# Low parts of the second halves by accumulating transfers, and eight more pieces by seven products, in an encoder block

## The chip, the cores and the metric

The kernel runs on one core of one Trainium2 chip. The metric is the time of one execution in microseconds of the device; what is compared is the median over several runs.

## The reference

One encoder block on 256 tokens of width 2048, in float32:

```
h    = rms_norm(x) @ w_in                       # q, k, v of two attentions, and two gates
ya   = windowed_gqa(...)   ; yb = dilated_attention(...)
x    = x + (sigmoid(ga) * (ya @ w_branch_a) + sigmoid(gb) * (yb @ w_branch_b)) @ w_out
hf   = rms_norm(x)
x    = x + (gelu(conv3(hf @ w_ffn_gate)) * (hf @ w_ffn_up)) @ w_ffn_down     # d_ff 5632
x    = x + sigmoid(rms_norm(x) @ w_ple_gate) * (p @ w_ple_proj)
out  = rms_norm(x)
```

Nearly all of the work is products of 256 rows with weight matrices, whose float32 weights are read from memory once.

## The kernel before, in words

**Pieces, units, parts.** The weights lie in memory as 258 pieces of 1 MB (128 partitions by 2048 float32). Each is loaded by SP (`load`) into one of three buffers `raw`. A matrix product is made from split operands: a float32 operand is written as a high part, rounded to the type that TensorE takes, and a low part, the rest; a product then is three matmuls, high by high, high by low, low by high (`thirds`, L408 to L410). ACT makes the high part of the weights (L305, an `ACTIVATE` Copy into `uh` or `vh`) and DVE the low part (L306, raw less high, into `ul` or `vl`). This is done by `produce`, a unit at a time; a unit is half a piece or less. Plain units go to rings of six slots (`uh`, `ul`), units of weight sums to rings of two (`vh`, `vl`). `drop` gives a slot back when the last product that reads it has been written, and `pump` then produces what has become possible, so production is some three pieces ahead of use.

**Stages.** A: input projection and attention. B0 to B3: the two gates, 512 columns of each at a time, with the branch projections ba and bb behind each. D0, D1: output projection. E0, E1: up and gate projections of the two halves of the inner width. F00, F01, F10, F11: down projections. pp0, pp1, G0, G2, G3: the embedding at the end. In A and E the weights are the stationary operand (L351, L358), and each piece takes 32 matmuls. In B, D, F and G0 (the quad stages) a piece is a 2 by 2 arrangement of 128x512 blocks, times 2 by 2 blocks of activations. A piece is of one of these kinds, given by a letter in the strings `FIRST_GATES` (B0), `ALT` (B1 to B3, D, and G0 with Z for S) and `DOWN` (F0, F1):

- `s`: by eight block products, 24 matmuls.
- `S`: by seven (Winograd's form of Strassen's method), 21 matmuls. DVE forms the sums of weight blocks in place in `raw` (L295 to L297), and sums of activation blocks are made once and kept (`combine`, `sums_of`). Its units are a first quarter, a second half, and two units of sums.
- `Z`: by seven, with one sum of weights made beforehand: POOL loads three blocks by halves (`sum_ahead`, L268), DVE adds (L271, L272), POOL stores (L275), all during E0 and E1, and the later load fetches 768 KB of the piece and 256 KB of the sum. DVE does L282 and L283 in place.
- `w`: branch projections, and G2 and G3, by plain products, 24 matmuls.

A planner sets the order of instructions on each engine before the run; it may put ready matmuls ahead of others. What is wrapped in `keep` stays in program order on its engine. `at(stage, ...)` and `run_due` hang side work (sums of activations, row sums, transposes) at places in the product order.

Of the kernel before, what the change touches and what calls it, by code (L numbers as in the profile page):

```python
# [16 lines left out]
P = 128  # L17
# [74 lines left out]
WIDE = 2 * T  # L92
_JOBS = _plan()
NA = len(_JOBS)
ALT = "SsSsSsSs"
DOWN = ("ZZsZsZsZsZs", "ZsZsZsZsZss")
LASTS = 30
ASK, ADD, STORE = 0, 12, 13
FIRST_GATES = "ssssSsSs"


def _ffn(half):
# [65 lines left out]
def _unit_list():  # L168

    units, of = [], []  # L170
    for p, (kind, _) in enumerate(_PIECES):
        if p == 0:
            cuts = [("n", a * P, b * P) for a, b in ((0, 1), (1, 4), (4, 7), (7, 11), (11, PIECE))]
        elif kind == "Z":
            cuts = [("n", WIDE, 2 * WIDE), ("n", 2 * WIDE, 4 * WIDE), ("T21", 0, 2 * WIDE), ("T03", 2 * WIDE, 4 * WIDE)]
        elif kind == "S":
            cuts = [("n", 0, WIDE), ("n", 2 * WIDE, 4 * WIDE), ("T13", 0, 2 * WIDE), ("T24", 2 * WIDE, 4 * WIDE)]
        else:
            cuts = [("n", 0, 2 * WIDE), ("n", 2 * WIDE, 4 * WIDE)]
        of.append(list(range(len(units), len(units) + len(cuts))))  # L180
        units += [(p, *cut) for cut in cuts]
    return units, of


_UNITS, _UNITS_OF = _unit_list()
_FBLOCKS = [(u, o) for p, (kind, _) in enumerate(_PIECES) if kind == "f" for u in _UNITS_OF[p]
            for o in range((_UNITS[u][3] - _UNITS[u][2]) // P)]
_LAST_OF = {u: o for u, o in _FBLOCKS}
# [5 lines left out]
def _encoder(ctx: ExitStack, tc, xt, pt, xrow, cols, gainrow, table, onehot, mask, ident_in, wts, out):  # L194
# [84 lines left out]
    def sums_of_weights(raw):  # L279

        q = [raw[:, i * WIDE:(i + 1) * WIDE] for i in range(4)]
        nc.vector.tensor_tensor(q[1], q[0], q[1], op=ALU.subtract)  # L282
        nc.vector.tensor_tensor(raw[:, 2 * WIDE:], raw[:, 2 * WIDE:], view(q[0], 0, (0, 2), (1, WIDE)), op=ALU.subtract)  # L283

    def produce():

        u = state["unit"]
        p, kind, a, b = _UNITS[u]
        while state["raw"] < min(p + 3, _NPIECES):
            load(state["raw"])  # L290
        raw = raws[p]
        ring = "u" if kind == "n" else "v"
        if kind == "T13":
            q = [raw[:, i * WIDE:(i + 1) * WIDE] for i in range(4)]
            nc.vector.tensor_tensor(raw[:, :2 * WIDE], raw[:, WIDE:3 * WIDE], raw[:, :2 * WIDE], op=ALU.subtract)  # L295
            nc.vector.tensor_tensor(q[2], q[2], q[0], op=ALU.subtract)
            nc.vector.tensor_tensor(q[3], q[3], q[2], op=ALU.subtract)  # L297
        behind = _PIECES[p][0] == "Z" == _PIECES[p - 1][0]
        if kind == "T21" and not behind:
            sums_of_weights(raw)  # L300
        src = raw[:, a:b]
        pool = wpool if ring == "u" else held["tok"]
        hi = pool.tile([P, b - a], FR, name=ring + "h", bufs=RINGS[ring])
        lo = pool.tile([P, b - a], FR, name=ring + "l", bufs=RINGS[ring])
        nc.scalar.activation(hi, src, AF.Copy)  # L305
        nc.vector.tensor_tensor(lo, src, hi.bitcast(F32), op=ALU.subtract)  # L306
        if behind and u == _UNITS_OF[p][1]:
            sums_of_weights(raw)
        made[u] = (hi, lo)
        state["unit"] = u + 1  # L310
        state[ring] -= 1
# [275 lines left out]
    def at(i, f, *a):  # L587

        due.setdefault(i, []).append((f, a))
# [320 lines left out]
    def sums_of(u, tag, s=None):  # L910

        tok = held["tok"]
        f = tok.tile([P, 4, P], F32, name="cmb")
        x11, x21, x12, x22 = (u[:, k, t * P:(t + 1) * P] for k in range(2) for t in range(2))
        nc.vector.tensor_tensor(f[:, 0], x21, x22, op=ALU.add)
        nc.vector.tensor_tensor(f[:, 2], x11, x21, op=ALU.subtract)
        nc.vector.tensor_tensor(f[:, 1], f[:, 0], x11, op=ALU.subtract)
        nc.vector.tensor_tensor(f[:, 3], x12, f[:, 1], op=ALU.subtract)
        if s is None:
            s = tok.tile([P, 2, 4, P], FR, name="S", tag="S%d" % tag)  # L920
        nc.scalar.activation(s[:, 0], f, AF.Copy)
        nc.vector.tensor_tensor(s[:, 1], f, s[:, 0].bitcast(F32), op=ALU.subtract)
        return s
# [36 lines left out]
        return h  # L960

    at(("B0", 3, 0), open_tok)
    for i, when in ((4, (3, 1)), (6, (3, 6)), (0, (5, 2)), (2, (7, 2))):
        at(("B0", *when), combine, "hs", hs, i, i // 2)
    rh = halved(rc[0])

    for j in range(4):

        def gated(t, n, a):
            c = held["c"][t][:, cut[n]]  # L970
            nc.vector.tensor_tensor(c, a, c, op=ALU.add)
            a = c
            nc.scalar.activation(c, a, AF.Tanh, scale=rh[:, t:t + 1])

        if j == 1:
            at(("ba1", 0, 0), combine, "merged", held["merged"], 0, 4)
        if j == 3:
            at(("B3", 2, 4), combine, "merged", held["merged"], 2, 0)
            at(("B3", 4, 4), combine, "merged", held["merged"], 4, 1)
        quads("B%d" % j, lambda k: hs[:, k, :], lambda i: combos["hs", i], gated)  # L980
        if j == 0:
            held["merged"] = big.tile([P, KC, 2 * T], FR, name="merged", tag="R1")
        c = held["c"]
        for half, (stage, y, names) in enumerate((("ba%d" % j, lambda k: ya[:, k, :], ("M1", "M6")), ("bb%d" % j, yb.get, ("M7", "M5")))):
            accs = wide_stage(stage, y, names)
            for t in range(2):
                m = c[t][:, cut[half]]
                nc.vector.scalar_tensor_tensor(m, m, 1.0, accs[t], op0=ALU.add, op1=ALU.mult)
                if half:
                    nc.vector.tensor_tensor(c[t][:, cut[0]], c[t][:, cut[0]], m, op=ALU.add)  # L990
        merged_turns("B%d" % (j + 1) if j < 3 else "D0", j, c)
# [7 lines left out]
    def residual(stage, s, moving, key, square):  # L999

        wide = slice(2 * s * WIDE, 2 * (s + 1) * WIDE)

        def finish(t, n, a):
            r = xr[:, t, cut[2 * s + n]]
            nc.vector.tensor_tensor(r, r, a, op=ALU.add)
            if n:
                nc.vector.tensor_tensor(xr[:, t, wide], xr[:, t, wide], held["c"][t], op=ALU.add)
            if n and square:
                nc.scalar.activation(held["c"][t], xr[:, t, wide], AF.Square,
                                     accum_out=held["ssq"][:, s, t:t + 1])  # L1010

        quads(stage, moving, lambda i: combos[key, i], finish)
# [127 lines left out]
    for half in range(2):  # L1140
        held["act"], held["places"] = {}, places(half)
        jobs = _ffn(half)
        joint = 0 if half else JOINT
        stage = "E%d" % half
        accs = [bank(which) for which in ("M1", "M5", "M6", "M7")[:joint]]
        if joint:
            products(stage, lambda k: hf[:, k, :], KC, accs)
        for (kind, n), a in zip(jobs, accs):
            mlp(kind, n, a)
        turns["e"] = 0  # L1150
        todo = [(p, h) for p in sevens(half) for h in range(2)]
        for i, (kind, n) in enumerate(jobs[joint:]):
            if i > 1 and todo and (i % 2 == 0 or i < LASTS):
                held["job"] = todo.pop(0), ("act2", "S4")[i % 2]
                one_ahead(stage)
            finish_ahead(stage)
            mlp(kind, n, product(stage, lambda k: hf[:, k, :], KC, "e"))
        assert not todo
        drain_ahead()
        if half:  # L1160
            at(("F10", 2, 0), load_last)
            at(("F10", 9, 0), split_last)
            held["ssq"] = sc.tile([P, 2, 2], F32, name="ssq", bufs=1)
        residual("F%d0" % half, 0, activation_row, "act", half)
        if half:
            pl = big.tile([P, KC, 2 * T], FR, name="pl", tag="R0")
            for pair, when in enumerate((("F11", 0, 6), ("F11", 1, 2), ("F11", 1, 5), ("F11", 2, 1))):
                at(when, rows_pair, "P22", pair, pl, 2)
            at(("F11", 2, 4), combine, "pl", pl, 0, 0)
            at(("F11", 4, 4), combine, "pl", pl, 2, 1)  # L1170
        residual("F%d1" % half, 1, activation_row, "act", half)


# [8 lines left out]
        held["rp"] = halved(rows_root())  # L1182

    at(("pp1", 0, 0), ple_root)
    at(("pp1", 0, 4), combine, "pl", pl, 4, 2)
    at(("G0", 1, 4), combine, "pl", pl, 6, 3)
    names = ("M1", "M6", "M7", "M5")

    class Rows:
# [118 lines left out]
```

## Time and profile before

| | |
|---|---|
| times of three runs | 1455.38, 1455.40, 1455.77 us |
| median | 1455.4 us |
| span of the profiled execution (first to last instruction) | 1453.7 us |
| TensorE matmuls | 7470 |
| pieces by seven in B0, B1 to B3, D0, D1, G0 | 2, 4 each, 4, 4, 4 |
| pieces by seven in F00, F01, F10, F11 | 6, 6, 5, 5 of 11 |
| DMA read from memory and written to it | 299.94 MB, 8.95 MB |

The profile is of one execution. Its own time outside the profiler is not recorded apart from the three runs; the span lies 1.7 us below their median. PE is TensorE's matmul, PEld its weight load, DVE VectorE, ACT ScalarE, POOL GpSimd, SP the engine whose queue issues the weight loads. A `q` behind an engine's name is its instruction queue. A group of instructions shows line, engine, operation, what it writes and reads, the shape, the count, then busy us, mean ns of one, and idle time before them with what ended it. In a timeline a row begins with start and duration in us. Rows of a stretch give its bounds, its length, the busy time of PE, PEld, DVE, ACT and POOL with their counts, the granted clock of TensorE, the mean busy share of the sixteen DMA engines and GB/s.

### The profile page before, as it was taken

The numbers are of one execution on the slowest core, as the hardware profiler recorded it, in microseconds if no ns is written. First come the engines' busy times: TensorE is split into PE (matmuls) and PEld (weight loads), VectorE is DVE, ScalarE is ACT, GpSimd is POOL, SyncE is SP. The second block draws the span as 40 slices with busy tenths as digits, with TensorE's granted clock in tenths as the row PEclk, the third lists the DMA queues.
The fourth block names the chain that finished last, engine by engine and source line by source line (L and its number), as shares of the span: only waits on it lengthen the run. The fifth ranks groups of instructions, "written<-read, shape, count | busy, mean of one in ns | idle before, by whom it ended". The sixth has DMA issues, their size and how long they took to land.

```text
span 1453.7 us, 19747 instructions
## 1 busy us (share of the span) xinstructions
PE 1442.7 (99%) x7470; PEld 1234.0 (85%) x7470; DVE 1220.8 (84%) x1730; ACT 829.6 (57%) x1148; POOL 73.8 (5%) x113
## 2 busy tenths in 40 slices
PE   9999999999999999999999999999999999999997
PEld 8888888888888888888888888888888888888885
DVE  7677665679998989989877999997878799998994
ACT  7455544546555656566545566465545466555753
POOL 0000000000000000000221100000121200000000
PEclk9999999999999999999999999999999999999998
DMA  9753445435456456465767655566776765556462
GB/s 330 252 209 146 155 167 175 172 143 203 189 190 231 180 210 239 178 253 203 277 238 267 241 208 198 189 248 227 263 275 243 271 236 213 197 194 233 173 236 82
DMA packets 58522, 310.17 MB, mean 213 GB/s; under 512 B 7028, under 2 KB 12020, under 8 KB 29500
## 3 DMA queue, kind: packets, MB, share of 16 engines
q1 hardware_dynamic: 49388, 280.46, 53.1%
q0 software_dynamic: 8320, 27.27, 5.2%
q8 instruction: 58, 0.95, 0.3%
q10 hardware_dynamic: 720, 1.19, 0.2%
q14 instruction: 36, 0.29, 0.1%
HBM read 299.94 MB, written 8.95 MB: 212 GB/s over the span
## 4 chain that ended last, share of the span: by engine, by line
PE 98%; DMA 0%; issue 0%; DVE 0%; ACT 0%; SPq 0%; POOLq 0%; POOL 0%; DVEq 0%
PE bank L351 29%; PE bank L358 15%; PE bank L408 15%; PE bank L409 14%; PE bank L410 14%; PE bank L397 2%; PE bank L399 2%; PE bank L398 2%; PE bank L335 2%; PE bank L336 1%; PE bank L939 1%; PE bank L755 0%; PE bank L703 0%; PE bank L702 0%; PE bank L701 0%; DMA raw<-in_wts 0%
## 5 line engine op out<-in xcount | busy, mean ns | idle before, releaser
L305 ACT ACTIVATE uh<-raw 128x1024 fp32r<-128x1024 f32 (+2 forms) x519 | 518.1, 1010 | 297.0 <-PE bank L410 106.5
L306 DVE TENSOR_TENSOR ul<-raw,uh 128x1024 fp32r<-128x1024 f32 (+2 forms) x519 | 594.4, 1164 | 96.5 <-ACT uh L305 65.9
L351 PE MATMUL bank<-hf,uh 128*128 128x512 f32 x1408 | 336.3, 391 | 0.0
L351 PEld LDWEIGHTS bank<-hf,uh 128*128 128x128 f32 x1408 | 258.9, 188 | 50.1
L358 PEld LDWEIGHTS bank<-hf,ul 128*128 128x128 f32 x1408 | 180.4, 191 | 6.7
L358 PE MATMUL bank<-hf,ul 128*128 128x256 f32 x1408 | 182.8, 283 | 0.0
L305 ACT ACTIVATE vh<-raw 128x1024 fp32r<-128x1024 f32 x96 | 101.1, 1058 | 59.8 <-DVE raw L282 27.0
L306 DVE TENSOR_TENSOR vl<-raw,vh 128x1024 fp32r<-128x1024 f32 x96 | 116.3, 1220 | 1.1
L351 PE MATMUL bank<-hs,uh 128*128 128x512 f32 x432 | 103.6, 392 | 0.0
L351 PEld LDWEIGHTS bank<-hs,uh 128*128 128x128 f32 x432 | 79.5, 188 | 15.6
L410 PE MATMUL bank<-uh,act 128*128 128x512 f32 x218 | 84.9, 390 | 0.0
L409 PE MATMUL bank<-ul,act 128*128 128x512 f32 x218 | 84.8, 389 | 0.0
L408 PE MATMUL bank<-uh,act 128*128 128x512 f32 x218 | 84.6, 390 | 0.0
L496 ACT ACTIVATE t<-bank 128x256 f32<-128x256 f32 x122 | 45.3, 374 | 59.8 <-PE bank L358 48.7
L408 PE MATMUL bank<-uh,hs 128*128 128x512 f32 x172 | 67.4, 392 | 0.0
L410 PE MATMUL bank<-uh,hs 128*128 128x512 f32 x172 | 67.2, 391 | 0.0
L409 PE MATMUL bank<-ul,hs 128*128 128x512 f32 x172 | 67.0, 389 | 0.0
L1084 ACT ACTIVATE gw<-gw,cl 128x256 f32<-128x256 f32 x44 | 24.0, 594 | 72.2 <-DVE gw L1081 71.9
L271 DVE TENSOR_TENSOR ahead<-ahead 128x256 f32<-128x256 f32 x52 | 21.9, 422 | 46.8 <-DMA ahead<-in_wts 46.8
L268 POOL DMA_DIRECT2D ahead<-in_wts x52 | 39.0, 750 | 375.7 <-DMA ahead<-ahead 207.0
L358 PE MATMUL bank<-hs,ul 128*128 128x256 f32 x432 | 56.6, 284 | 0.0
L358 PEld LDWEIGHTS bank<-hs,ul 128*128 128x128 f32 x432 | 54.5, 191 | 1.0
(266 smaller groups left out, 2423.8 us busy)
## 6 DMA issues: line engine op xcount, KB each, us to landing
raw<-in_wts SPq DMA_DIRECT2D x225, 1024.0 KB, 4.9
ahead<-in_wts POOLq DMA_DIRECT2D x52, 384.0 KB, 5.2
raw<-in_wts SPq DMA_DIRECT2D x26, 768.0 KB, 5.1
ahead<-ahead POOLq DMA_DIRECT2D x52, 128.0 KB, 4.4
raw<-ahead SPq DMA_DIRECT2D x26, 256.0 KB, 4.9
raw<-in_wts SPq DMA_DIRECT2D x12, 512.0 KB, 7.0
xr<-in_xrow SPq DMA_DIRECT2D x4, 512.0 KB, 8.4
x<-in_xt SPq DMA_DIRECT2D x13, 128.0 KB, 6.0
```

What stands on the lines that cost most here:

```text
L268: keep(nc.gpsimd.dma_start(q, wts[p][:, :3 * WIDE].rearrange("p (q c) -> p q c", c=WIDE)[:, :, cols]))
L305: nc.scalar.activation(hi, src, AF.Copy)
L306: nc.vector.tensor_tensor(lo, src, hi.bitcast(F32), op=ALU.subtract)
L335: nc.tensor.matmul(acc, hi[:, w], m, start=first, stop=False, skip_group_check=True)
L351: nc.tensor.matmul(acc, weights(u)[0][:, o * P:(o + 1) * P], m, start=first, stop=False, skip_group_check=True)
L358: nc.tensor.matmul(acc[:, T:], weights(u)[1][:, o * P:(o + 1) * P], m[:, :T], start=False, stop=last, skip_group_check=True)
L397: nc.tensor.matmul(acc[:, :n * P], xh, hi, start=(k == 0), stop=False)
L398: nc.tensor.matmul(acc[:, :n * P], xh, lo, start=False, stop=False)
L408: nc.tensor.matmul(acc, sh, wh, start=first, stop=False)
L409: nc.tensor.matmul(acc, sh, wl, start=False, stop=False)
L410: nc.tensor.matmul(acc, sl, wh, start=False, stop=last)
L496: keep(nc.scalar.activation(t, acc[:, T:], AF.Copy, scale=scale))
```

## The change

The second unit of each piece in B, ba, bb, D, F and G0, whatever its kind, gets its low part in another way: ACT writes minus the high part into the slot of the low part, then the high part; then POOL issues a transfer that adds the weights to the slot. For `s` and `w` the transfer reads the weights from `raw`; for `S` and `Z`, whose `raw` is overwritten by sums, from memory. One more piece goes by seven products in each of B1, B2, B3, D0, D1, F10, F11 and G0. In B0 one of the two pieces by seven is another. The sums of activations follow; one set of them is held in a sixth place, the buffer `act2`. Where a piece by seven follows another in the list of pieces, its sums of weights are now formed just behind its second unit, for `S` as for `Z`.

```
-ALT = "SsSsSsSs"
-DOWN = ("ZZsZsZsZsZs", "ZsZsZsZsZss")
+ALT = "SsSSsSSs"
+DOWN = ("ZZsZsZsZsZs", "ZZsZsZsZsZs")
-FIRST_GATES = "ssssSsSs"
+FIRST_GATES = "sssssSSs"
...
+_MOVED = {_UNITS_OF[p][1] for stage in _STAGES if stage[0] in "BbDFG" and stage not in ("G2", "G3")
+          for p in _STAGES[stage] if _PIECES[p][0] in 'swSZ'}
...
+    def all_sums_of_weights(raw):
+
+        q = [raw[:, i * WIDE:(i + 1) * WIDE] for i in range(4)]
+        nc.vector.tensor_tensor(raw[:, :2 * WIDE], raw[:, WIDE:3 * WIDE], raw[:, :2 * WIDE], op=ALU.subtract)
+        nc.vector.tensor_tensor(q[2], q[2], q[0], op=ALU.subtract)
+        nc.vector.tensor_tensor(q[3], q[3], q[2], op=ALU.subtract)
...
-        behind = _PIECES[p][0] == "Z" == _PIECES[p - 1][0]
+        behind = _PIECES[p][0] in "SZ" and _PIECES[p - 1][0] in "SZ"
+        if kind == "T13" and not behind:
+            all_sums_of_weights(raw)
...
-        nc.scalar.activation(hi, src, AF.Copy)
-        nc.vector.tensor_tensor(lo, src, hi.bitcast(F32), op=ALU.subtract)
+        if u in _MOVED:
+            nc.scalar.activation(lo, src, AF.Copy, scale=-1.0)
+            nc.scalar.activation(hi, src, AF.Copy)
+            keep(nc.gpsimd.dma_start(lo, src if _PIECES[p][0] in "sw" else wts[p][:, a:b], accum_op=ALU.add))
+        else:
+            nc.scalar.activation(hi, src, AF.Copy)
+            nc.vector.tensor_tensor(lo, src, hi.bitcast(F32), op=ALU.subtract)
         if behind and u == _UNITS_OF[p][1]:
-            sums_of_weights(raw)
+            (sums_of_weights if _PIECES[p][0] == "Z" else all_sums_of_weights)(raw)
...
-    for i, when in ((4, (3, 1)), (6, (3, 6)), (0, (5, 2)), (2, (7, 2))):
-        at(("B0", *when), combine, "hs", hs, i, i // 2)
+    for i, when, tag in ((5, (3, 6), 2), (6, (4, 5), 3), (0, (5, 5), 0), (2, (6, 5), 1), (3, (7, 2), 5)):
+        at(("B0", *when), combine, "hs", hs, i, tag)
...
-            at(("B3", 4, 4), combine, "merged", held["merged"], 4, 1)
+            at(("B3", 4, 4), combine, "merged", held["merged"], 3, 1)
+            at(("B3", 7, 4), combine, "merged", held["merged"], 5, 5)
...
+            at(("F11", 6, 4), combine, "pl", pl, 3, 2)
...
-    at(("pp1", 0, 4), combine, "pl", pl, 4, 2)
-    at(("G0", 1, 4), combine, "pl", pl, 6, 3)
+    at(("pp1", 0, 4), combine, "pl", pl, 5, 3)
+    at(("G0", 1, 4), combine, "pl", pl, 6, 4)
```

More of the change, by code (lines that the diff above doesn't have):

```diff
@@ L292, in produce @@
         ring = "u" if kind == "n" else "v"
[L293 to L297, printed above, removed]
-        behind = _PIECES[p][0] == "Z" == _PIECES[p - 1][0]
+        behind = _PIECES[p][0] in "SZ" and _PIECES[p - 1][0] in "SZ"
+        if kind == "T13" and not behind:
+            all_sums_of_weights(raw)
         if kind == "T21" and not behind:
@@ L919, in sums_of @@
         if s is None:
-            s = tok.tile([P, 2, 4, P], FR, name="S", tag="S%d" % tag)
+            s = tok.tile([P, 2, 4, P], FR, name="S", tag="S%d" % tag if tag < 5 else "act2")
         nc.scalar.activation(s[:, 0], f, AF.Copy)
```

## The prediction

> **What bounds the kernel now.** I read the page first: shares of engines, the chain that ended last, the queues.
>
> ```profile
> span 1453.7 us, 19747 instructions
> PE 1442.7 (99%) x7470; PEld 1234.0 (85%) x7470; DVE 1220.8 (84%) x1730; ACT 829.6 (57%) x1148; POOL 73.8 (5%) x113
> q1 hardware_dynamic: 49388, 280.46, 53.1%
> q0 software_dynamic: 8320, 27.27, 5.2%
> PE 98%; DMA 0%; issue 0%; DVE 0%; ACT 0%; SPq 0%; POOLq 0%; POOL 0%; DVEq 0%
> ```
>
> The chain of work that ended last is 98% TensorE. As a busy PE need not be PE at its peak, I looked next at what its weight loads waited for (line, releaser, total, times, longest); the longest rows are:
>
> ```profile
> PEld bank L408 <- ACT vh L305: 1.4, 4, 0.4
> PEld bank L939 <- DVE c L990: 1.1, 4, 0.3
> PEld bank L336 <- DVE ul L306: 1.1, 3, 0.5
> ```
>
> No wait sums to more than 1.4 us. So time is lost or won through the number of matmuls, unless the change brings PE a wait. The cadence, from the timeline of PE where a B1 piece by eight begins (403.28 is its first product, 403.96 the first with the second half's weights):
>
> ```profile
> 403.28 0.39 PE L408 MATMUL bank<-uh,hs 128*128 128x512 f32 x1
> 403.51 0.39 PE L409 MATMUL bank<-ul,hs 128*128 128x512 f32 x1
> 403.74 0.39 PE L410 MATMUL bank<-uh,hs 128*128 128x512 f32 x1
> 403.96 0.39 PE L408 MATMUL bank<-uh,hs 128*128 128x512 f32 x1
> 404.19 0.39 PE L409 MATMUL bank<-ul,hs 128*128 128x512 f32 x1
> ```
>
> Four starts in 0.91 us: one matmul in 0.2275 us, one product (three matmuls) in 0.68, a piece by eight in 5.46 and one by seven in 4.78. What stands beside it, stage by stage, from the stretches (us, busy time of PE, weight loads, DVE, ACT and POOL, granted clock, DMA share, GB/s): B, D, F0, F1, then E1 and G0.
>
> ```profile
> 304.00:542.00 238.00, 238.00 (x1080) 196.73 (x1079) 221.00 (x278) 137.26 (x159) 0.00 (x0) 1.00 0.51 189
> 542.00:627.00 85.00, 85.00 (x382) 68.67 (x381) 82.02 (x99) 52.51 (x62) 0.00 (x0) 1.00 0.60 221
> 870.00:988.00 118.00, 118.00 (x527) 97.33 (x526) 111.28 (x125) 66.84 (x75) 0.61 (x1) 1.00 0.58 214
> 1232.00:1346.00 114.00, 114.00 (x510) 94.26 (x509) 105.17 (x125) 66.27 (x80) 0.00 (x0) 1.00 0.58 212
> 990.00:1231.00 241.00, 241.00 (x1390) 213.13 (x1389) 200.40 (x328) 133.43 (x196) 35.50 (x54) 1.00 0.69 244
> 1357.00:1400.00 43.00, 43.00 (x190) 35.36 (x190) 39.74 (x55) 26.44 (x33) 1.08 (x1) 1.00 0.66 242
> ```
>
> DVE is at 92 to 96% in the quad stages, so it is what keeps more pieces from going by seven; ACT (56 to 62%) and the DMA engines (0.51 to 0.66) have room.
>
> **The change, part by part.** *Products.* Eight pieces (one each in B1, B2, B3, D0, D1, F10, F11, G0) lose one product of three matmuls: 24 x 0.2275 = 5.46 us of PE. This is the only term on the path.
>
> *DVE and ACT.* Durations (mean ns behind the busy time):
>
> ```profile
> L306 DVE TENSOR_TENSOR vl<-raw,vh 128x1024 fp32r<-128x1024 f32 x96 | 116.3, 1220 | 1.1
> L305 ACT ACTIVATE vh<-raw 128x1024 fp32r<-128x1024 f32 x96 | 101.1, 1058 | 59.8 <-DVE raw L282 27.0 <-PE bank L410 11.9 <-DVE raw L297 8.6
> L295 DVE TENSOR_TENSOR raw<-raw 128x1024 f32<-128x1024 f32 x22 | 26.9, 1222 | 0.3
> L296 DVE TENSOR_TENSOR raw<-raw 128x512 f32<-128x512 f32 x22 | 15.1, 685 | 0.0
> L271 DVE TENSOR_TENSOR ahead<-ahead 128x256 f32<-128x256 f32 x52 | 21.9, 422 | 46.8 <-DMA ahead<-in_wts 46.8
> ```
>
> The moved units are one per piece: B 32, branches 12, D 16, F 44, G0 8, together 112. DVE loses 112 x 1.22 = 136.6 us. A piece turned to sevens gives it back 1.5 more subtractions of 1024 (1.83) and the sums of weights (1.22 + 2 x 0.685 = 2.59, less one 0.685 for a Z piece): some 4.2 x 8 = 34 us; four more sums of activations, each two steps of 512 and four small ones, about 2.5, 10 us; six more half sums ahead, two steps each, 5 us. Net about -88 us: DVE near 1133 us. Within B (44 units) it falls from 221 to 221 - 53.7 + 3 x 4.4 + 5 = about 185 of 236, 79%. ACT gains 112 copies x 1.058 = 118.5 and 12 units' worth for the sevens, 13: near 963 us, 66%; in B 137 + 46.6 + 5 = 189 of 236, 80%. All of it beside PE, costed at nothing; the cover is PE's own work. If it went, a B stage would show ACT over its 57 us, which needs another 10 us in each.
>
> *The transfers.* Each adds 512 KB to what ACT wrote. The trace shows none that accumulates. Nearest rows (KB each, us from issue to landing; and the POOL instructions' min/median/max ns):
>
> ```profile
> raw<-in_wts SPq DMA_DIRECT2D x225, 1024.0 KB, 4.9
> raw<-in_wts SPq DMA_DIRECT2D x44, 1024.0 KB, 6.2
> ahead<-in_wts POOLq DMA_DIRECT2D x52, 384.0 KB, 5.2
> ahead<-ahead POOLq DMA_DIRECT2D x52, 128.0 KB, 4.4
> L268 POOL DMA_DIRECT2D ahead<-in_wts x52: 741/743/929, 638.8 to 1168.4; - x52
> DMA to landing us min/median/max: 2.7/5.0/8.9
> ```
>
> (The second row is the stretch of B alone, the last all raw loads.) Landing lies between 4.4 and 8.9 us. I take 5.5, a little over POOL's own 384 KB row, and keep the ends. POOL is in order: behind a transfer that waits for ACT's copy stand the next transfers, at the end of E1 the last loads and stores of sums ahead, at the start of the embedding's second piece the power for the norm. 112 x about 0.65 us is 73 us more POOL time at 5% load; hidden. SP is in order too: a load into a buffer that a transfer still reads waits, and later loads behind it.
>
> How much room is there? The same B1 piece by eight, as ACT and DVE made it, and ACT's first copy of the piece three later, which uses the same raw buffer:
>
> ```profile
> 391.87 1.06 ACT L305 ACTIVATE uh<-raw 128x1024 fp32r<-128x1024 f32 x1 [0.19 <-DMA raw<-in_wts]
> 393.28 1.06 ACT L305 ACTIVATE uh<-raw 128x1024 fp32r<-128x1024 f32 x1 [0.36 <-PE bank L410]
> 394.46 2.35 DVE L306 TENSOR_TENSOR ul<-raw,uh 128x1024 fp32r<-128x1024 f32 x2
> 408.35 1.04 ACT L305 ACTIVATE uh<-raw 128x1024 fp32r<-128x1024 f32 x1
> ```
>
> The second half's slot is free at 393.28; DVE had the low part at 396.81; PE reads it at 404.19. Now the low copy ends at 394.34, and the transfer may take 9.85 us. By 5.5 it lands at 399.8, 4.3 us early. It also holds the raw buffer until then, 3 us longer: the next load lands 6.2 us on, at 406.0, before 408.35. This second room is gone at a landing of 7.8 us. Sevens read memory instead of the buffer, and PE reads their second half last, 2.7 us later in the piece than a piece by eight does: more room.
>
> The Trainium skill's page "SBUF — State Buffer", section "Who interferes with whom", says that DVE's two-port modes lock GpSimd out while it writes descriptors, which would speak against transfers from POOL beside a busy DVE. The row above agrees with its remark that a two-input subtraction has no such mode: 743 ns is the median and 929 the longest of 52.
>
> *Neighbours by seven.* Sevens' sums have two slots; the next piece's must be made in the five products (3.4 us) between a slot's release and its next use, for which ACT and DVE need 1.06 + 1.22 = 2.28 us. Such pairs go from 2 (heads of F00, F01) to 17. At the head of F00:
>
> ```profile
> 876.27 1.06 ACT L305 ACTIVATE vh<-raw 128x1024 fp32r<-128x1024 f32 x1 [0.99 <-PE bank L410]
> 879.50 1.22 DVE L306 TENSOR_TENSOR vl<-raw,vh 128x1024 fp32r<-128x1024 f32 x1
> 880.36 0.84 PE L408 MATMUL bank<-vh,S 128*128 128x512 f32 x3
> ```
>
> 4.45 us from start to end, DVE being busy elsewhere, and yet weight loads waited for vh 1.4 us in the whole span: the order put three matmuls with the high part (L408) in a row, ahead of those that need the low one. With DVE relieved I cost it at nothing; the bound is 15 x 0.4 = 6 us.
>
> *Sum.* 1453.7 - 5.5 = 1448.2 us of span; the median of the runs, 1455.4, lies 1.7 us above this execution's span, so 1450.0.
>
> **The rivals.** *The DMA engines become the bound (slower).* 221 GB/s at a share of 0.60 makes 368 GB/s full use, so 512 KB moved once take 1.42 us of all sixteen engines, and the 112 raise the quad stages to 0.78 (B, 0.51 + 44 x 1.42 / 236), 0.87 (D), 0.85 (F) and 0.93 (G0): it fits. If an accumulating transfer costs twice that, because its target is read as well, the same stages need 1.04, 1.14, 1.11 and 1.20 of their time: 9 + 12 + 25 + 9 = about 55 us over, less 5.5, 1505. But single slices of D's stretch moved more than 368:
>
> ```profile
> GB/s 416 366 15 0 35 339 413 208 0 31 351 302 331 390 280 361 225 405 284 174 393 416 15 0 0 0 31 359 355 243 0 0 216 355 409 15 39 274 386 401
> ```
>
> At 416 full use the four are 0.92, 1.01, 0.98 and 1.06, some 3 us over. So this case gives 1453 to 1505, in the middle 1480; it decides once transfers land later than 7.8 us (raw buffers) and surely at 9.85 (PE waits in every piece by eight, 44 of them, and 12 branch pieces). For it: loads already come in pairs that fill the engines; against it: half of each stage's slices are nearly idle. The Trainium skill's page "Collectives: The Full Stack", section "The bandwidth ceiling: the fold count and why AG ≠ RS ≠ AR", states that an add on the way needs two source reads and so halves the rate; that is this rival, and no run here shows it yet.
>
> *The pairs of sevens cost what they save (no change).* 15 new pairs at 0.35 us are 5.3 us: 1455. For it: the room is 1.1 us and ACT goes to 80%; against it: the F00 rows above.
>
> *PE is helped beyond its count (a little faster still).* In D DVE is at 96% and would go to 88% (82.0 - 19.5 + 8.8 + 2.5 of 84 us); a us or two of hesitation on PE could come back: 1448. The waits on record sum to too little to expect it.
>
> **How the numbers follow.** Forecast 1450.0, with helped PE, 0.52 (own range 1447 to 1452.5); pairs 0.16; DMA bound 0.32. 0.2% (2.9 us) is about what a measurement tells from no change here. Faster 0.52, same 0.16, slower 0.32. The range runs from 1447 to 1482: a few hundredths lie below, and the upper half of the DMA case, 0.16, above.
>
> **What would show it.** Right: 7446 matmuls; PE at 99%; DVE near 1133 us, ACT near 963; 112 transfers of 512 KB on POOL landing in 5 to 6 us; no wait of weight loads on a DMA. The pairs: weight loads waiting for vh or vl by more than 5 us in all. The DMA case: landings of 8 us and more, DMA slices at 9 through the quad stages, ACT waiting for raw loads far more than before, PE below 98%. The prediction fails if an accumulating transfer takes longer than a plain load of twice its size.

## The result and the profile after

The changed kernel takes 1601.8 us (median; 1596.6 to 1609.0) against 1455.4 for the kernel before: ratio 1.101, 95% interval 1.098 to 1.104. Forecast were 1450.0 us and a range of 1447 to 1482: the sign and the size are both wrong. The page of the changed kernel, its span, TensorE and the two DMA queues, and the chain that ended last:

```profile
span 1598.1 us, 20204 instructions
PE 1488.7 (93%) x7446; PEld 1247.7 (78%) x7446; DVE 1148.7 (72%) x1691; ACT 938.7 (59%) x1281; POOL 179.4 (11%) x237
q1 hardware_dynamic: 49820, 280.46, 50.0%
q0 software_dynamic: 25408, 89.14, 24.8%
PE 60%; DMA 23%; ACT 5%; issue 5%; DVE 5%; SPq 0%; POOL 0%; POOLq 0%; ACTq 0%; DVEq 0%
```

The counts are those forecast (7446 matmuls; DVE 1149 us, forecast 1133; ACT 939, forecast 963). What changed is the chain: 98% TensorE before, 60% now, and 23% DMA. POOL's queue, q0, went from 5.2% to 24.8% of the sixteen engines. Next the waits (line, releaser, total, times, longest) and the DMA issues (KB each, median us to landing):

```profile
PEld bank L420 <- DMA ul<-raw: 70.3, 28, 5.7
PEld bank L420 <- DVE vl L317: 17.3, 18, 2.0
PEld bank L419 <- ACT vh L316: 12.0, 9, 2.5
PEld bank L420 <- DMA ul<-in_wts: 5.1, 3, 2.6
ACT uh L316 <- DMA raw<-in_wts: 201.7, 83, 7.9
```

```profile
raw<-in_wts SPq DMA_DIRECT2D x222, 1024.0 KB, 5.6
ul<-raw POOLq DMA_DIRECT2D x56, 512.0 KB, 7.8
ul<-in_wts POOLq DMA_DIRECT2D x56, 512.0 KB, 8.2
```

TensorE now waits 70 us for transfers from the buffers and 5 us for those from memory, though the latter land later: a piece by seven reads its second half last. ACT waits 202 us for raw loads (41.5 before). The stretches of the quad stages (us, busy time of PE, weight loads, DVE, ACT, POOL, granted clock, DMA share, GB/s): B, D, F0, F1, G0.

```profile
304.00:592.00 288.00, 254.07 (x1070) 200.99 (x1069) 192.35 (x260) 178.19 (x210) 38.47 (x44) 0.96 0.89 239
592.00:693.00 101.00, 88.62 (x379) 69.01 (x378) 78.49 (x97) 66.95 (x82) 12.22 (x14) 0.97 0.93 269
940.00:1086.00 146.00, 124.17 (x497) 98.31 (x496) 82.81 (x91) 80.95 (x90) 17.29 (x20) 0.93 0.87 235
1331.00:1480.00 149.00, 126.31 (x510) 98.20 (x509) 98.72 (x131) 95.36 (x118) 19.57 (x23) 0.93 0.89 235
1496.00:1545.00 49.00, 43.52 (x179) 33.83 (x178) 31.76 (x41) 31.72 (x40) 6.17 (x7) 0.97 0.89 253
```

They last 733 us. Before, the same five lasted 598; 6 of these belong to E (its last matmul starts at 874.7, the stretch of F0 begins at 870), and 5 less are needed now: 587. A and E keep their length. The DMA shares, 0.51 to 0.66 before, are 0.87 to 0.93, and length times share is 256 + 94 + 127 + 133 + 44 = 653 us of full use: of the 146 us over, some 66 would be lost even with engines that are never idle. The other 80 are idle engines beside a TensorE that waits or runs slowly. How that comes about is seen at the border of B2 to B3 (start, us, engine, line, operation; idle before it):

```profile
488.27 25.05 SPq L259 DMA_DIRECT2D raw<-in_wts  x6
...
495.49 1.06 ACT L316 ACTIVATE uh<-raw 128x1024 fp32r<-128x1024 f32 x1 [7.04 <-DMA raw<-in_wts]
...
502.08 1.05 ACT L312 ACTIVATE ul<-raw 128x1024 fp32r<-128x1024 f32 x1
...
503.53 0.86 POOL L314 DMA_DIRECT2D ul<-raw  x1 [3.81 <-ACT ul L312]
...
508.80 0.39 PE L419 MATMUL bank<-uh,yb 128*128 128x512 f32 x1
512.43 0.79 PE L420 MATMUL bank<-ul,yb 128*128 128x512 f32 x1 [3.24 <-DMA ul<-raw]
513.02 0.63 PE L421 MATMUL bank<-uh,yb 128*128 128x512 f32 x1
```

ACT stood idle 7 us until a load landed; its copies followed, the transfer went out at 503.53 and landed at 512.38, 8.85 us later, and TensorE, which started its last matmul at 508.80, had stopped at 509.19. Then it ran slowly, as the stretches around that wait show (columns as above, the clock last but two):

```profile
508.00:512.40 4.40, 1.19 (x6) 0.65 (x4) 3.68 (x4) 3.00 (x4) 0.00 (x0) 0.88 1.01 209
512.40:518.00 5.60, 5.57 (x13) 4.42 (x14) 2.15 (x4) 0.81 (x1) 0.87 (x1) 0.50 1.01 296
518.00:521.00 3.00, 3.00 (x14) 2.40 (x14) 1.11 (x2) 1.81 (x3) 0.00 (x0) 0.96 0.99 287
```

Granted clock 0.50 for 5.6 us: from the second on, its matmuls start 0.427 us apart instead of 0.2275. Counted over the trace, by the starts of neighbouring 512-column matmuls: 51 gaps over 1 us lose 100 us, 24 smaller ones 10, 139 matmuls at about half pace (0.38 to 0.48 us apart) 28, and some hundred slightly long steps (0.28 to 0.38 us) 10, of which the kernel before has 57 that lose 5. That is some 147 us, the size of the loss.

### The profile page after: what moved, and what is told of

Read it like the earlier page. It is cut to its first block, busy times and chain, and to the rows that moved or that the text cites. A ratio compares the mean times of both kernels' runs of the same rounds, so it can differ in the third digit from the quotient of the medians.

```text
span 1598.1 us, 20204 instructions
## 1 busy us (share of the span) xinstructions
PE 1488.7 (93%) x7446; PEld 1247.7 (78%) x7446; DVE 1148.7 (72%) x1691; ACT 938.7 (59%) x1281; POOL 179.4 (11%) x237
## 3 DMA queue, kind: packets, MB, share of 16 engines
q0 software_dynamic: 25408, 89.14, 24.8%
## 4 chain that ended last, share of the span: by engine, by line
PE 60%; DMA 23%; ACT 5%; issue 5%; DVE 5%; SPq 0%; POOL 0%; POOLq 0%; ACTq 0%; DVEq 0%
PE bank L362 26%; DMA raw<-in_wts 15%; PE bank L369 13%; DMA ul<-raw 7%; PE bank L420 4%; PE bank L421 4%; PE bank L419 4%; DVE vl L317 2%; PE bank L408 2%; PE bank L410 2%; PE bank L409 2%; PE bank L346 1%; ACT uh L316 1%; ACT vh L316 1%; DVE ul L317 1%
## 5 line engine op out<-in xcount | busy, mean ns | idle before, releaser
L317 DVE TENSOR_TENSOR ul<-raw,uh 128x1024 fp32r<-128x1024 f32 (+2 forms) x407 | 458.1, 1139 | 249.7 <-ACT uh L316 216.1
L316 ACT ACTIVATE uh<-raw 128x1024 fp32r<-128x1024 f32 (+2 forms) x407 | 398.8, 990 | 374.8 <-DMA raw<-in_wts 201.7
L317 DVE TENSOR_TENSOR vl<-raw,vh 128x1024 fp32r<-128x1024 f32 x112 | 135.5, 1221 | 27.4 <-ACT vh L316 26.6
L316 ACT ACTIVATE vh<-raw 128x1024 fp32r<-128x1024 f32 x112 | 116.5, 1051 | 18.9 <-DVE raw L292 7.5
L312 ACT ACTIVATE ul<-raw 128x1024 fp32r<-128x1024 f32 x112 | 117.1, 1047 | 3.6 <-PE bank L369 2.6
L313 ACT ACTIVATE uh<-raw 128x1024 fp32r<-128x1024 f32 x112 | 117.3, 1047 | 2.8 <-PE bank L362 1.9
L314 POOL DMA_DIRECT2D ul<-raw x56 | 49.0, 875 | 576.7 <-ACT ul L312 270.9
L314 POOL DMA_DIRECT2D ul<-in_wts x56 | 48.9, 873 | 336.7 <-ACT ul L312 271.1
L420 PEld LDWEIGHTS bank<-ul,act 128*128 128x128 f32 x208 | 42.4, 204 | 48.0 <-DMA ul<-raw 39.1
L419 PE MATMUL bank<-vh,S 128*128 128x512 f32 x120 | 50.9, 425 | 19.7 <-ACT vh L316 8.0
```

Source lines behind the costliest of these rows:

```text
L312: nc.scalar.activation(lo, src, AF.Copy, scale=-1.0)
L314: keep(nc.gpsimd.dma_start(lo, src if _PIECES[p][0] in "sw" else wts[p][:, a:b], accum_op=ALU.add))
L419: nc.tensor.matmul(acc, sh, wh, start=first, stop=False)
L420: nc.tensor.matmul(acc, sh, wl, start=False, stop=False)
```

## The experiments

Three theories stood at first. A: the transfers' time on the DMA engines. B: place and holding, late landings keep raw buffers, so loads, copies and the next transfers come late. C: the neighbouring pieces by seven. Later expectations say theirs anew.

**e1, the changed kernel without transfers** (the low part stays minus the high part).

```
-            keep(nc.gpsimd.dma_start(lo, ..., accum_op=ALU.add))
```

> The changed kernel without its 112 accumulating transfers (the low parts of the second halves are then minus the high parts: the weights are not added). Theory A, the transfers' own engine time: the trace of the changed kernel puts 24.8% of 1598 us on POOL's queue; less the sums ahead (5.2% of 1453.7 us for 52, so 84 us for 58) that is 312 us for 112, 2.79 us of all sixteen engines each, twice the 1.42 us of 512 KB moved once. Without them the DMA share falls back to 0.5 to 0.7 and the time to 1448 to 1455. Theory B, the place of the transfers (raw buffers held and low parts late, whatever a transfer costs): the same, 1448 to 1455. Theory C, seventeen pairs of neighbouring pieces by seven on two slots: most of the loss stays, above 1530.

Measured: 1460.6 us, ratio 1.0025 (1.0014 to 1.0035). So all but some 5 us of the loss hangs on the transfers, and C falls as the main cause. But 24 matmuls fewer should have given 1450. F10 took 64.0 us where its products need 56. Its waits there, and the stretch:

```profile
PE bank L418 <- DVE pair L510: 4.1, 2, 2.5
PEld bank L418 <- ACT t L506: 2.9, 1, 2.9
```

```profile
1218.00:1283.00 65.00, 59.35 (x267) 48.48 (x266) 49.77 (x69) 48.34 (x62) 1.87 (x3) 0.97 0.59 217
```

Six more half sums made ahead stand in the tail of E1, and the gate's last steps on ACT and DVE come late: two of the stops in F10 (2.5 and 1.6 us) wait for `pair`, a third of 1.6 us waits for the sums of the second piece by seven (`vl`).

**e2, plain copies instead of accumulating ones.**

```
-accum_op=ALU.add
```

> The same 112 transfers, with the same sources, targets, waits and order, but they copy instead of adding (the low part is then the whole weight). Theory A: a copy takes about 1.42 us of the engines instead of 2.79, the quad stages need 0.78 to 0.93 of the DMA engines, and most of the loss goes: 1450 to 1485. Theory B: landing shortens only by the second read, from about 8 to about 6 us, the holds and waits stay, and so does more than half of the loss: 1530 or more. Theory C: 1580 or more.

Measured: 1513.8 us, ratio 1.040 (1.037 to 1.043). Half-way, and neither theory foresaw it. The queue and the transfers' landings (changed kernel: 24.8%; 7.8 us):

```profile
q0 software_dynamic: 25408, 89.14, 16.9%
```

```profile
ul<-raw POOLq DMA_DIRECT2D x56, 512.0 KB, 5.7
```

What a transfer costs follows from the queue's share. Sums ahead took 0.052 x 1453.7 = 75.6 us for 104 transfers, so 84 for the 116 here. An accumulating transfer: (0.248 x 1598.1 - 84) / 112 = 2.79 us of all sixteen engines. A copy: (0.169 x 1510.6 - 84) / 112 = 1.53. That does not come from the crowd: with twelve transfers alone (e14) the same sum gives (0.076 x 1454.9 - 75.6) / 12 = 2.9. The prediction's 1.42 was about right for a copy. The Trainium skill's page "Collectives: The Full Stack", section "The bandwidth ceiling: the fold count and why AG ≠ RS ≠ AR", says of collective operations that an add on the way reads two sources and so halves the rate; the trace agrees in the main, 2.79 to 1.53, a factor of 1.8. Taking the second read away gave 88 us (1601.8 to 1513.8); the copies that stay cost 53 over e1.

**e3, the transfers alone**, on the pieces of the kernel before.

```
+_MOVED = ...   # 112 units, as changed
+        if u in _MOVED: ... accum_op=ALU.add ...
```

> The kernel before with the 112 transfers, and its own patterns of pieces by seven and by eight (no eight more by seven). Theories A and B: the transfers cost what they cost in the changed kernel, 140 to 160 us over 1455: 1575 to 1610. Theory C: no new pairs of neighbours, so within 15 us of 1455.

Measured: 1581.7 us, ratio 1.084 (1.081 to 1.087); weight loads wait as they do in the changed kernel:

```profile
PEld bank L416 <- DMA ul<-raw: 78.3, 30, 4.9
```

So transfers alone cost 126 us.

**e4, transfers only for pieces by seven** (56, all from memory).

```
-          for p in _STAGES[stage] if _PIECES[p][0] in 'swSZ'}
+          for p in _STAGES[stage] if _PIECES[p][0] in 'SZ'}
```

> The changed kernel with transfers only in the pieces by seven: 56, all read from memory, so none holds a raw buffer; the pieces by eight and the branch pieces have their low parts from DVE again. Theory A: the DMA engines are needed for 0.72 of B's time (121 + 17 x 2.79 of 233 us), 0.94 of D, 0.91 of F and about 1.0 of G0, so B is free of loss and D, F and G0 lose some: 1455 to 1500. Theory B: no raw buffer is held and PE reads these halves last in a piece: 1450. Theory C: 1560 or more.

Measured: 1493.9 us, ratio 1.025 (1.022 to 1.028). The loss lies in single places. B1 (first row) took 50.6 us for 41; F00 and F01 (second row) lost nothing:

```profile
366.00:410.00 44.00, 38.43 (x161) 30.61 (x160) 34.98 (x44) 27.13 (x31) 3.49 (x4) 0.90 0.79 231
870.00:985.00 115.00, 115.00 (x545) 96.72 (x544) 98.00 (x115) 77.98 (x92) 9.54 (x11) 1.00 0.84 245
```

The stage that loses has the lower share: a share by itself decides nothing. Weight loads hardly wait for transfers here (2.6 us in all). They wait for the sums of weights, and each of these waits over 0.5 us stands in the second of two neighbouring pieces by seven:

```profile
PEld bank L419 <- ACT vh L316: 15.7, 6, 5.3
```

The longest of these waits makes up most of the loss in B1: TensorE stood idle for 4.9 us until 403.99, and thirteen matmuls at half pace followed.

**e5, all transfers from memory**, so that none holds a raw buffer.

```
-lo, src if _PIECES[p][0] in "sw" else wts[p][:, a:b]
+lo, wts[p][:, a:b]
```

> The changed kernel, but the 56 transfers of plain and branch pieces also read their weights from memory, so that no transfer holds a raw buffer and the next load need not wait for a landing. Number, size and engine time of the transfers stay (2.79 us of all sixteen engines each). Theory A (the engines' time is short, and loads and transfers delay each other whoever waits for whom): 1590 to 1612 us, B1 to B3 still 48 us and more. Theory B (the loop is closed by the held buffer: late landing, late next load, late copies, later landing): the loop is open, the waits of ACT for raw loads fall below 100 us in all and the time to 1540 or less.

Measured: 1576.4 us, ratio 1.083 (1.081 to 1.085). ACT's wait for loads fell as B had said, the time only by 25 us. The waits, and B's stretch:

```profile
ACT uh L316 <- DMA raw<-in_wts: 88.9, 59, 5.3
PEld bank L420 <- DMA ul<-in_wts: 82.8, 37, 7.1
```

```profile
304.00:562.00 258.00, 243.11 (x1065) 193.71 (x1064) 190.59 (x260) 179.48 (x211) 38.45 (x44) 0.99 0.97 266
```

In B the held buffers were what left engines idle: without them the share is 0.97, and 288 us become 258. Then the engines themselves are the bound: 258 x 0.97 = 250 us of work, more than the 236 us of products. In F little was won (F0 146 to 139, F1 149 to 150).

**e6, transfers of half the width**, DVE making the other half.

```
+            keep(nc.gpsimd.dma_start(lo[:, :WIDE], ..., accum_op=ALU.add))
+            nc.vector.tensor_tensor(lo[:, WIDE:], src[:, WIDE:], hi[:, WIDE:].bitcast(F32), op=ALU.subtract)
```

> The changed kernel, but each of the 112 transfers adds only the first 512 of the unit's 1024 columns; DVE makes the low part of the other 512. The engines' time of the transfers halves (about 156 us in all, that of the 112 plain copies, which ran in 1513.8 us), DVE gets 112 x 0.69 = 77 us back (near 1226). Theory A (engine time decides): 1500 to 1525 us. Theory B (number of transfers, held buffers and the fixed part of a landing decide): over two thirds of the loss stays, 1555 or more. If DVE at 84% with its new sums becomes a bound as well, small waits on vl of 5 to 10 us come on top in either case.

Measured: 1531.8 us, ratio 1.052 (1.051 to 1.054). Between the bands, nearer to A: half the engine time, (0.171 x 1531.5 - 84) / 112 = 1.59 us each, leaves 71 of 141 us over e1.

```profile
q0 software_dynamic: 25408, 59.78, 17.1%
```

**e7, no transfers, and F10 and F11 as before.**

```
-DOWN = ("ZZsZsZsZsZs", "ZZsZsZsZsZs")
+DOWN = ("ZZsZsZsZsZs", "ZsZsZsZsZss")
-            keep(nc.gpsimd.dma_start(lo, ..., accum_op=ALU.add))
```

> The changed kernel without its transfers (the low parts of the second halves stay minus the high part), and with F10 and F11 in the order of pieces of the kernel before (five by seven of eleven, no longer six sums made ahead in the tail of E1). Matmuls 7452, 18 fewer than before, worth 4.1 us. Theory (the run without transfers lost 8 to 9 us only at the border of E1 to F10, because E1's tail has six more half sums and the head's sums to make): 1451.6 us, 1450 to 1453; F10 at 56 to 57 us instead of 64. Rival (the loss at F10 comes from the pairs of sevens or from the embedding's later sums): F10 stays above 60 and the time at 1456 to 1460.

Measured: 1453.9 us (1452.4 to 1457.8), ratio 0.999 (0.998 to 0.9999). F10 is at 56.7 us and TensorE at 99% again. The edit takes away four of the six more half sums and, with them, the pair of sevens at the head of F10; one of the two, or both, cost F10 its 8 us. The stops seen in e1 point at both, and they were not separated. Of the 4.1 us for 18 matmuls 1.5 are left in the median, 2.9 in the span:

```profile
PE 1438.7 (99%) x7452; PEld 1230.3 (85%) x7452; DVE 1132.3 (78%) x1669; ACT 934.3 (64%) x1275; POOL 76.6 (5%) x117
```

**e8, POOL subtracts** in the place of copy and transfer, in the order of e7.

```
-            nc.scalar.activation(lo, src, AF.Copy, scale=-1.0)
-            keep(nc.gpsimd.dma_start(lo, ..., accum_op=ALU.add))
+            nc.gpsimd.tensor_tensor(lo, src, hi.bitcast(F32), op=ALU.subtract)
```

> The same order of pieces as the run before this one, but complete: the low parts of the second halves are subtracted by POOL (raw less high, 128x1024) instead of copied and added by a transfer. No DMA beyond that of the kernel before, no second copy on ACT. No row of any run shows such a subtraction on POOL. If it takes up to 3 us and leaves DVE alone, 8 units in a stage of 41 us fill POOL to 60%: hidden, 1452 us (1450 to 1454), below the kernel before. If it takes 5 us or more, POOL is full in every quad stage: 1480 or more. If it slows DVE's subtractions (1.22 us) beside it, they lengthen in the rows and vl comes late: 1456 to 1475.

Measured: 1585.4 us, ratio 1.088 (1.086 to 1.091), far over the 1456 to 1475 us expected for a subtraction of up to 3 us that slows DVE. By its mean of 2.8 us the subtraction fits, but DVE's own became longer beside it (mean ns: vl 1220 and raw 1221 in e7; here POOL's group, then DVE's in B), and weight loads waited 44 us for vl. What share of the 130 us each of the two has was not separated:

```profile
L313 POOL TENSOR_TENSOR ul<-raw,uh 128x1024 fp32r<-128x1024 f32 x112 | 314.9, 2818 | 729.0 <-ACT uh L312 431.2 <-PE bank L368 245.0 <-DVE ul L316 48.2
```

```profile
L316 DVE TENSOR_TENSOR vl<-raw,vh 128x1024 fp32r<-128x1024 f32 x34 | 51.8, 1537 | 3.3 <-ACT vh L315 3.2
L290 DVE TENSOR_TENSOR raw<-raw 128x1024 f32<-128x1024 f32 x18 | 32.5, 1803 | 0.5
```

The Trainium skill's page "SBUF — State Buffer", section "Who interferes with whom", says that a DVE instruction with two inputs in SBUF contends with a GpSimd instruction that reads SBUF; 1221 ns grown to 1803 agree.

**e9, the eight more pieces by seven alone**, all low parts by DVE.

```
-          for p in _STAGES[stage] if _PIECES[p][0] in 'swSZ'}
+          for p in _STAGES[stage] if _PIECES[p][0] in ''.split()}
```

> The changed kernel with its eight more pieces by seven, but without transfers: DVE makes every low part, as in the kernel before. DVE's work comes to 1149 + 112 x 1.22 = 1285 us; in a stage like B1 it needs 38.4 (before) + 4.4 = 42.8 us for 41.4 us of products: 103%, so 1.5 us over in each of B1 to B3 and D0, D1, G0, 9 us in all, F10's head (8 to 9 us without transfers) and 5.5 us saved: about 1468 us, 1460 to 1480, waits of the weight loads on vl and ul made by DVE, none on a DMA. Rival: DVE's queue has room in the stages between (A, E, branches) and takes the excess: 1458 to 1461, as the run without transfers.

Measured: 1477.8 us, ratio 1.0155 (1.014 to 1.017), inside the range expected, but not in the places expected. B1 and its branches (first row) keep their time with DVE at 99%; the loss begins in D (second row), where DVE is still at 98%, and F10's head has its own:

```profile
361.50:420.00 58.50, 58.50 (x263) 47.98 (x262) 57.69 (x70) 35.18 (x42) 0.00 (x0) 1.00 0.53 201
535.00:636.00 101.00, 94.88 (x405) 74.03 (x404) 98.53 (x119) 56.29 (x70) 0.00 (x0) 0.97 0.52 191
```

With e3 this makes a square: pieces alone +23 us, transfers alone +126, both +146. The transfers bought next to nothing of what the pieces cost.

**e10, plain copies, all from memory.**

```
-lo, src if _PIECES[p][0] in "sw" else wts[p][:, a:b], accum_op=ALU.add
+lo, wts[p][:, a:b]
```

> The 112 transfers as plain copies, all read from memory: no second read, no held raw buffer (the low parts of the second halves then are the weights themselves). With accumulation the same step, from buffer to memory, gave 25 us of 1602. Theory A (engine time): the engines' time is that of the plain copies that read half from the buffers, 1513.8 us; so 1500 to 1520. Theory B (held buffers make the rest of the loss): 1465 to 1490, ACT's waits for raw loads near those without transfers.

Measured: 1519.1 us, ratio 1.043 (1.040 to 1.045), so no better than e2. In the sum, held buffers cost something only with the second read; the copies' 53 us are not theirs. B is the exception: B1 to B3 took 43.0 to 44.2 us, in e2 44.0 to 46.9.

**e11 and e12, two and one transfer a stage** in B1 to B3, D0, D1 and G0, F10 and F11 as before.

```
+_MOVED = {_UNITS_OF[p][1] for stage in ("B1", "B2", "B3", "D0", "D1", "G0")
+          for p in [p for p in _STAGES[stage] if _PIECES[p][0] in 'SZ'][1:4:2]}   # e12: [2:3]
```

> Eight-stage version with few transfers: F10 and F11 in the old order, and accumulating transfers (from memory) only for the second half of the second and the fourth piece by seven in each of B1, B2, B3, D0, D1 and G0, 12 in all; DVE makes the other low parts. 7452 matmuls, 4.1 us fewer than before; DVE in B1 at 38.4 + 4.4 - 2.4 = 40.4 of 41.4 us. Theory (each transfer beside loads delays the loads of its neighbours by its engine time and the loss grows with their number): 2 x 2.8 us of the engines in a stage, about 2 us lost in each of the six, less 4.1: 1463 us, 1456 to 1470. Rival (threshold: a stage with DMA share 0.51 to 0.66 takes 5.6 us more without a wait): 1451 to 1453, below the kernel before.

> As the run before, with one transfer in each of the six stages, for the third piece by seven: 6 in all. DVE in B1 at 38.4 + 4.4 - 1.2 = 41.6 of 41.4 us. By the dose theory the transfers cost half as much, 1 us in a stage, and DVE at 100% something on top: 1456 to 1462. By the threshold rival the transfers cost nothing and DVE decides: 1452 to 1458.

Measured: 1465.0 us, ratio 1.006 (1.004 to 1.008), and 1468.9 us, 1.009 (1.008 to 1.011). Fewer transfers were not faster, so their number does not decide; the two medians are 3.9 us apart, and the profile of e11 is of its slowest run (1470.7 us). With one transfer, B1 to B3 ran at 41.1 to 41.4 us and D1 at 53.5; with two, D1 at 47.0, but B1 at 43.5. What D1 lost with one transfer hangs in good part on a single stop until that transfer landed, 8.2 us after its issue, and on the half clock behind it:

```profile
PEld bank L420 <- DMA ul<-in_wts: 4.9, 1, 4.9
```

So even one transfer in a stage can cost something where DVE is nearly full; whether DVE's delay or the landing comes first was not tried.

**e13, five pieces by seven in B1 to B3 alone**, on the kernel before (B0's pieces and the place of the sums as in the changed one).

```
+FIVE = "SsSSsSSs"
-... ALT if j else FIRST_GATES)
+... (FIVE if j in (1, 2, 3) else ALT) if j else FIRST_GATES)
```

> The kernel before with one part of the change alone: five instead of four pieces by seven in B1, B2 and B3 (and the other second piece in B0), no transfers, everything else as before. 7461 matmuls, 9 fewer, worth 2.0 us. In the run with all eight more pieces by seven and no transfers, B1 to B3 ran at 41.3 to 41.4 us (41.8 to 42 before) with DVE at 98 to 99%, and the loss began in D. Theory (the gain of the products is real, and DVE's cover decides where it may be taken: D keeps four here): 1453.5 us, 1452 to 1455. Rival (DVE leaves B late and D, at 96% already, pays for it): D0 and D1 above 44 us each, 1456 to 1462.

Measured: 1458.0 us, ratio 1.0021 (1.0012 to 1.0030): slower, as the rival had it, though only D1 went over its 44 us. B2 fell from 42.0 to 41.4 us, D0 stayed at 42.0, but D1, its pieces unchanged, went from 43.8 to 47.1. D's stretch, before and here:

```profile
535.00:627.00 92.00, 92.00 (x413) 74.47 (x412) 88.98 (x108) 56.24 (x66) 0.00 (x0) 1.00 0.58 208
```

```profile
535.00:627.00 92.00, 90.09 (x399) 71.42 (x398) 87.86 (x106) 52.47 (x65) 0.00 (x0) 1.00 0.54 200
```

By the same time DVE and ACT have done less of D's work than before: they come to it late, and TensorE's waits there are on ul, vl and uh (1.4, 1.4 and 1.3 us).

**e14, twelve transfers alone**, for the pieces by seven of F00 and F01.

```
+_MOVED = {_UNITS_OF[p][1] for stage in ("F00", "F01") for p in _STAGES[stage] if _PIECES[p][0] == "Z"}
```

> The kernel before with 12 accumulating transfers alone: the second halves of the pieces by seven in F00 and F01, read from memory, no other change. In the run with transfers for all pieces by seven these two stages showed no loss (55.9 and 55.8 us) at a DMA share of 0.83. Theory (a transfer costs PE nothing where landings, copies and loads still come in time, whatever the engines' share): 1455.4, within 2 us of the kernel before. Rival (the cost goes with the engines' time, 0.3 to 0.45 us a us of it as in the runs with 112): 12 x 2.79 x 0.37 = 12 us, 1465 to 1470.

Measured: 1456.5 us, ratio 1.0012 (1.0001 to 1.0024). The two stages (before: 52.20 and 56.08 us of DVE, share 0.56 and 0.58):

```profile
870.00:926.00 56.00, 56.00 (x255) 46.58 (x254) 45.81 (x56) 38.83 (x46) 5.14 (x6) 1.00 0.90 256
926.00:985.00 59.00, 58.23 (x256) 47.58 (x255) 48.25 (x52) 35.66 (x39) 4.29 (x5) 1.00 0.87 255
```

```profile
ul<-in_wts POOLq DMA_DIRECT2D x12, 512.0 KB, 8.3
```

F00 loses nothing at a share of 0.90 and landings of 8.3 us, where the changed kernel, with eleven transfers in each, took 67 to 79 us for the 56 of its F stages at 0.87 to 0.89. F01 loses 1 us. Eleven transfers in 56 us would need 0.57 x 56 + 11 x 2.79 = 63 us of the engines, so six are about what they have room for. No version that computes the whole block was faster than the kernel before.

## Why the prediction was wrong

*The transfers: the step that failed.* The prediction took a landing of 5.5 us and 1.42 us of engine time, from the rows of plain loads, for a kind of transfer that no row showed. Measured are 7.8 and 8.2 us, and 2.79. Its own conditions were good: the room of the raw buffers was to end at a landing of 7.8 us, and 7.8 is the median. It also said what would make it fail, an accumulating transfer longer than a plain load of twice its size: 7.8 against 5.6. The two values had both been laid out; the choice went to the row that looked nearest in size, not in kind.

*The DMA rival: right in mechanism, mis-sized.* It priced the excess at 55 us at full use, as the stretches bear out (66). It had no term for the rest: engines idle beside a waiting TensorE, in B because raw buffers are held (e5, 30 us there), and the halved clock. 55 was therefore a lower bound used as an upper one; 146 was measured. Setting 416 GB/s against it, and 1480 in the middle, had no support in a sustained stretch: none of the five moved over 269.

*The clock, 28 us, stood in no part.* In the changed kernel all but one of the waits from 2.9 us on (from one matmul's start to the next) brought half pace for some 2 to 6 us, and so did one of 2.32 us and some pairs of shorter waits close together (1.44 and 1.26 us); one of 3.38 us did not. The trace's clock record shows the pattern behind this. The clock changes on a fixed grid of 3.41 us, and each slow spell lasts one or two steps of it. By the starts and ends of the matmuls, TensorE was idle for 1.81 us or more in each of the 18 steps that end in a fall of the clock, and for at most 1.79 us in every other step at full clock. The border lies between 1.78 and 1.90 us in all sixteen traces. Here are the wait of 3.38 us, which the grid cuts in two, and the wait of 2.32 us, which falls into one step, each with the step behind it (idle 1.79 and 1.93 us by the busy time of PE):

```profile
1023.39:1026.80 3.41, 1.62 (x8) 1.00 (x6) 1.90 (x2) 1.54 (x3) 0.00 (x0) 1.00 0.95 213
1026.80:1030.21 3.41, 2.21 (x10) 1.82 (x11) 1.23 (x1) 1.98 (x3) 0.86 (x1) 1.00 1.02 221
1528.56:1531.97 3.41, 1.48 (x7) 0.98 (x6) 1.23 (x1) 3.38 (x4) 0.03 (x1) 1.00 1.02 286
1531.97:1535.38 3.41, 3.41 (x10) 2.37 (x9) 2.02 (x2) 2.39 (x3) 0.84 (x1) 0.50 1.06 210
```

The Trainium skill's page "TensorE: Matmul & The Clock Gate", section "HAM oscillation — how this bites in real kernels", warns of just this, DMA waits that put each next step at the low clock. It gives about 3.4 us for the window; many waits here were shorter than that and did it.

*Products.* The count was right and "the only term on the path" wrong. Without transfers the border of E1 to F10 took 8 us back (e1, e7); in kernels where DVE makes the low parts the gain turned into a loss in D (e9, e13). The step that booked six more half sums as 5 us of DVE beside TensorE, and the new pairs at nothing, counted their time, and not what stands behind them at the border of two stages.

*Engines beside PE.* DVE and ACT came out as sized. *Pairs of sevens.* Nearly free while loads come in time, F10's head perhaps excepted: e1 shows 3.9 us of waits on vl. Beside the transfers they are not: weight loads wait 29 us for vh and vl in the changed kernel and 24 in e4, but 7 in e3, which has the transfers and only the two old pairs. On top of the transfers the eight more pieces by seven cost 20 us (e3 to changed), without them 5 (e1). *Sevens have more room:* right for the transfers themselves, 5 us of waits against 70.

*Open:* the copies' 53 us (e2, e10) at stage shares near 0.8. That five transfers in B1 cost 9 us (e4) where six in F00 cost none goes with the pairs of sevens in B1; whether it is the pair, or that its sums are formed in the buffer and not made ahead, was not tried.

## What to carry to other kernels

Price a transfer by its kind, not its size: one that accumulates occupied the DMA engines 1.8 times as long as a copy, and where only a bound is known, the forecast should stand at the end that no row excludes. When work moves to a shared resource, compare each stage's demand on it with the stage's length. Here no stage's DMA share went beyond 0.97; some stages lost time near 0.8 (e2, e4), one lost none at 0.90 (e14). To a full stage, add the price of the waits themselves and of the half clock behind them. An engine at 96% that keeps up is no proof of room: work added in one stage was paid here in a later one that had none (e13).

## What had not been expected of the hardware

A subtraction of 128x1024 on POOL took 2.8 us, and DVE's sums beside it 1.8 us instead of 1.2 (e8). And the issue of an accumulating transfer on POOL took longer than that of a plain copy between the same buffers, 875 ns (changed kernel) against 533 (e2):

```profile
L314 POOL DMA_DIRECT2D ul<-raw x56 | 49.0, 875 | 576.7 <-ACT ul L312 270.9
L314 POOL DMA_DIRECT2D ul<-raw x56 | 29.9, 533 | 565.6 <-ACT t L507 250.0
```
